# HGRN heads: six groups of small-block products issued as one run behind the last decayed tile

## The chip, the cores and the metric

The kernel runs on one NeuronCore of a Trainium2 chip. The metric is the device time of one execution in microseconds; before the change it is the median of three runs, 1376.57 us (1376.02 to 1377.64).

## What is computed

A two-layer streaming encoder over 512 tokens of width 1024. Layer 0 mixes tokens with a gated DeltaNet, layer 1 with an HGRN2 gated linear recurrence, each followed by a squared-ReLU MLP of width 4096 and all of it in float32. The change is in the token mixer of layer 1:

```python
def _hgrn2_chunked(q, k, v, g):
    """S_t = diag(f_t) S_{t-1} + k_t v_t^T (k_t = 1 - f_t), o_t = S_t^T q_t.
    q,k,g (B,T,H,DK) with g = log f_t <= 0; v (B,T,H,DV). float32."""
...
    def step(S, xs):
...
        a_off = jnp.einsum('bhsik,bhsjk->bhsij', q_off, k_off)
        dec = jnp.exp(jnp.where(diag_mask[:, :, None],
                                gs[..., :, None, :] - gs[..., None, :, :], -jnp.inf))
        a_diag = jnp.einsum('bhsik,bhsjk,bhsijk->bhsij', qs, ks, dec)
```

There are 8 heads of 128 features. For each head a matrix `a` is wanted, which holds for every pair of tokens s <= t inside a chunk the product of q at t with k at s, each feature decayed by the forget gates between s and t. `o` is then `a` times v plus what the carried state S gives.

## The kernel before

Activations lie transposed, 128 features on the partitions and the 512 tokens along the free axis, and a head's 512 tokens are 4 chunks of 128 (`NC`).

**Projections.** All big products are "three-term" ones: weights and activations are split into a rounded high part and a low rest, and TensorE does hi*hi, hi*lo and lo*hi (lines 122 to 124, one output block of 128 x 512; lines 674 to 676 for v, with tokens on the partitions and 256 columns). The weights arrive by DMA (`weights`, L105), ScalarE casts the high part (L111) and VectorE subtracts the low one (L112).

**The HGRN stage** (`hgrn`, L595) goes through the heads in four pairs. While a pair's heads are worked (`hgrn_head`), the projections of the next pair (`hgrn_in`) and the output gates of an earlier one (`hgrn_gates`) are there to fill TensorE. Heads are written inside `high_priority(offset=3000)`. The order in which each engine gets its instructions is made when the kernel is built: a scheduler plays the program through with its own costs and gives each engine the ready instruction of highest priority. On the chip each engine runs its list in that order and waits at an instruction until its inputs are there.

**One head** (`hgrn_head`, L696). `g` holds the log gates. Two tiles `dk`, `dq` (four VectorE multiplies, L719) give products inside pairs of tokens. After a running sum over 64 tokens (L740), five levels (`HLEVELS`, block lengths 2, 4, 8, 16, 32) each make one decayed tile `e`: two VectorE subtracts (L747, L748), one exp on ScalarE (L749, recorded at L85), two VectorE multiplies (L750, L751). Left halves of the blocks carry k, right halves q, so that `e` against itself gives the cross products of one level.

For `dk`, `dq` and for the levels 2 to 16, `gram32` (L726) issues one group: 16 products of 128 x 32 by 128 x 32, one for each 32-token block of each chunk, which use a 32-column strip of the array (`tile_position`); float32 products show as two records each, so a group is 32 records. Each group is followed on VectorE by the masking multiply (L735) or a predicated copy into `ad` (L754). Level 32 issues a sixth group of 8 products (L760, 16 records) that ScalarE copies into `a` (L763). GpSimd copies `ad` into the diagonal blocks of `a` (L765). Each group takes a PSUM tile of its own from the ring `mb`, which has three.

Then `qf` and `kg`, the tiles decayed over whole 64-token blocks, are made (L769 to L779). L783 multiplies them for the cross of the two 64-token blocks of each chunk: four products with 64 columns of `kg` as the stationary side and 64 of `qf` as the moving one. ScalarE copies the result into `a` (L784). Scalings (L788), transposes (L791), the state updates (L796 to L803) and the outputs (L808, L810) follow. `ol`, the ring of work tiles from which `half`, `dk`, `dq`, the five `e`, `qf`, `kg` and `kt` come, has eight buffers.

**After the last pair** come a normalisation (`rstd_rows`, L183) and the output projection (`out_proj`, L821). Its first two weight tiles make four output blocks at once, three in the ring `pj` and the fourth in `mb`, and it takes the heads in order, so that only its last part needs head 7.

Of the kernel before, what the change touches and what calls it, by code (L numbers as in the profile page):

```python
# [15 lines left out]
ALU = mybir.AluOpType  # L16
PSUM = bass.MemoryType.PSUM

T, D, HID, NH, P = 512, 1024, 4096, 8, 128
NB = D // P  # L20
B = 32
MIX = {"ma": 2, "mb": 3}
NC = T // P
# [5 lines left out]
HLEVELS = (2, 4, 8, 16, 32)  # L29
# [3 lines left out]
class Net:  # L33
# [40 lines left out]
    def acc(self, shape=None):  # L74
        return self.pj.tile(shape or [P, T], F32, tag="pj", name=self.name("pj"))

    def after(self, i, prev):
        self.tc.add_manual_dep(
            i.ins, prev.ins.name,
            mybir.DependencyInfo(mybir.DependencyClass.NoSync, mybir.DependencyReason.DATA),  # L80
            reason="table order")

    def act(self, out, in_, func, **kw):

# [611 lines left out]
    def hgrn_head(self, h, kq, g, vt):  # L696
        nc, mm, ident = self.nc, self.nc.tensor.matmul, self.ident
        k, q = kq[:, 0], kq[:, 1]
        ck = lambda t, c: t[:, c * P:(c + 1) * P]
        hs = slice(h, h + 1)  # L700

        nc.gpsimd.tensor_scalar(out=g, in0=g, scalar1=1e-37, scalar2=self.oml[:, hs], op0=ALU.max, op1=ALU.mult)
        self.act(g, g, AF.Ln, bias=self.lb[:, hs])
        nc.scalar.activation(out=q, in_=q, func=AF.Copy, scale=self.oml[:, hs])
        tmp = lambda: self.work("ol", bufs=NH)
        gram = lambda: self.mix("gr", tag="mb")


        half = tmp()
        hv = half.rearrange("p (a n) -> p a n", a=2)  # L710
        gp = g.rearrange("p (n b) -> p n b", b=2)
        self.act(hv[:, 0], gp[:, :, 1], AF.Exp, scale=0.5)
        self.act(hv[:, 1], gp[:, :, 1], AF.Exp, scale=-0.5)
        dk, dq = tmp(), tmp()
        for dst, src, sg in ((dk, k, 0), (dq, q, 1)):
            d2, s2 = (t.rearrange("p (n b) -> p n b", b=2) for t in (dst, src))
            for b in (0, 1):
                e = nc.vector
                e.tensor_tensor(out=d2[:, :, b], in0=s2[:, :, b], in1=hv[:, (b + sg) % 2], op=ALU.mult)  # L719
        a = self.work("x" if h % 2 else "e")  # L720
        c4 = lambda t: t.rearrange("p (c t) -> p c t", c=NC)
        nc.gpsimd.memset(a, 0.0)
        blk = [slice(b, b + B) for b in range(0, P, B)]
        ad = self.work("wd" if h % 2 else "ud", [P, NC, B])

        def gram32(x, y):  # L726
            pa = self.mix("gr", [P, NC, B], tag="mb")
            for c in range(NC):
                for b in blk:
                    mm(pa[b, c], lhsT=ck(x, c)[:, b], rhs=ck(y, c)[:, b], start=True, stop=True,  # L730
                       tile_position=(0, b.start))
            return pa

        pa = gram32(dk, dq)
        nc.vector.tensor_tensor(out=ad, in0=pa, in1=self.dmask.unsqueeze(1).to_broadcast([P, NC, B]), op=ALU.mult)  # L735


        gc = g
        b64 = lambda t: t.rearrange("p (n s) -> p n s", s=64)
        nc.vector.tensor_tensor_scan(out=gc, data0=self.fresh, data1=g, initial=0.0, op0=ALU.mult, op1=ALU.add)  # L740

        for i, s in enumerate(HLEVELS):
            nb = T // (2 * s)
            v4 = lambda t: t.rearrange("p (n a s) -> p n a s", a=2, s=s)
            e = tmp()
            ref = v4(gc)[:, :, 0, s - 1:s].to_broadcast([P, nb, s])
            nc.vector.tensor_tensor(out=v4(e)[:, :, 0], in0=ref, in1=v4(gc)[:, :, 0], op=ALU.subtract)  # L747
            nc.vector.tensor_tensor(out=v4(e)[:, :, 1], in0=v4(gc)[:, :, 1], in1=ref, op=ALU.subtract)  # L748
            self.act(e, e, AF.Exp)  # L749
            nc.vector.tensor_tensor(out=v4(e)[:, :, 0], in0=v4(e)[:, :, 0], in1=v4(k)[:, :, 0], op=ALU.mult)  # L750
            nc.vector.tensor_tensor(out=v4(e)[:, :, 1], in0=v4(e)[:, :, 1], in1=v4(q)[:, :, 1], op=ALU.mult)  # L751
            if s < B:
                pa = gram32(e, e)
                nc.vector.copy_predicated(out=ad, mask=self.lmask[:, i + 1].unsqueeze(1).to_broadcast([P, NC, B]),  # L754
                                          data=pa)
                continue
            pa = self.mix("gr", [P, NC, B], tag="mb")
            for c in range(NC):
                for l, r in (blk[0:2], blk[2:4]):
                    mm(pa[l, c], lhsT=ck(e, c)[:, l], rhs=ck(e, c)[:, r], start=True, stop=True,  # L760
                       tile_position=(0, l.start))
            for l, r in (blk[0:2], blk[2:4]):
                nc.scalar.copy(out=c4(a)[l, :, r], in_=pa[l])  # L763
        for b in blk:
            nc.gpsimd.tensor_copy(out=c4(a)[b, :, b], in_=ad[b])  # L765


        qf, kg = tmp(), tmp()
        self.act(qf, gc, AF.Exp)  # L769
        last = self.work("last", [P, 2 * NC], bufs=2)  # L770
        egl = self.work("egl", [P, NC], bufs=2)
        nc.vector.tensor_copy(out=last, in_=b64(qf)[:, :, 63])
        lv = last.rearrange("p (c b) -> p c b", b=2)
        nc.vector.tensor_tensor(out=egl, in0=lv[:, :, 0], in1=lv[:, :, 1], op=ALU.mult)
        nc.vector.tensor_tensor(out=qf, in0=qf, in1=q, op=ALU.mult)
        nc.vector.tensor_tensor(out=b64(kg), in0=b64(gc)[:, :, 63:64].to_broadcast([P, 2 * NC, 64]), in1=b64(gc),
                                op=ALU.subtract)
        self.act(kg, kg, AF.Exp)
        nc.vector.tensor_tensor(out=kg, in0=kg, in1=k, op=ALU.mult)  # L779
        pa = gram()  # L780
        for c in range(NC):
            t = c * P
            mm(pa[0:64, t + 64:t + P], lhsT=kg[:, t:t + 64], rhs=qf[:, t + 64:t + P], start=True, stop=True)  # L783
        nc.scalar.copy(out=c4(a)[0:64, :, 64:P], in_=c4(pa)[0:64, :, 64:P])  # L784
        for t, half, n in ((kg, slice(0, 64), NC - 1), (qf, slice(64, P), NC)):
            v = c4(t)[:, 0:n, half]
            f = lv[:, 0:n, half.start // 64 ^ 1:(half.start // 64 ^ 1) + 1]
            nc.vector.tensor_tensor(out=v, in0=v, in1=f.to_broadcast([P, n, 64]), op=ALU.mult)  # L788
        pt = self.mix("pt", [P, NC - 1, P])
        for c in range(NC - 1):  # L790
            nc.tensor.transpose(pt[:, c], ck(kg, c), ident)  # L791
        kt = tmp()
        nc.scalar.copy(out=c4(kt)[:, 0:NC - 1], in_=pt)
        ps = self.mix("ps", [P, NC - 1, P])
        for c in range(NC - 1):
            mm(ps[:, c], lhsT=ck(kt, c), rhs=vt[:, c], start=True, stop=True)  # L796
        st = [None]
        for c in range(NC - 1):
            sn = self.work("s", [P, P], bufs=3)
            if c == 0:  # L800
                nc.vector.tensor_copy(out=sn, in_=ps[:, 0])
            else:
                nc.vector.scalar_tensor_tensor(out=sn, in0=st[c], scalar=egl[:, c:c + 1], in1=ps[:, c],  # L803
                                               op0=ALU.mult, op1=ALU.add)
            st.append(sn)
        po = self.mix("po")
        for c in range(NC):
            mm(ck(po, c), lhsT=vt[:, c], rhs=ck(a, c), start=True, stop=(c == 0))  # L808
            if c:
                mm(ck(po, c), lhsT=st[c], rhs=ck(qf, c), start=False, stop=True)  # L810
        on = self.on[h] = self.work("oh", bufs=NH)
        nc.scalar.copy(out=on, in_=po)
        self.square_into(h == 0, on, "v" if h >= NH - 1 else "g")
# [194 lines left out]
```

## Time and profile before

| what | value |
|---|---|
| median of three runs | 1376.57 us (1376.02 to 1377.64) |
| the profiled execution's own time | 1375.37 us |
| its span in the trace | 1373.3 us |
| mean granted TensorE clock | 0.996 |
| HGRN heads, start of the first group (L730) and of the last (L760) | 758.4 and 964.1 us |
| records of L730, L760, L783 | 1280, 128, 64 |

Times inside the trace are microseconds from the span's start, durations of single instructions in nanoseconds where it says so. PE is TensorE's matmul row, PEld its weight loads, DVE VectorE, ACT ScalarE, POOL GpSimd. In a timeline row the first number is the start, the second the length from the first start to the last end of the merged instructions, then engine, line, operation, output and inputs, shapes and the count; brackets hold the idle time of the engine before it and what ended it. Matmuls are pipelined: one of 512 columns shows about 400 ns, while the next starts some 230 ns after it. So what a thing costs TensorE is read from starts, not from lengths. In a row of a group of instructions, the numbers behind the bar are the busy time, the mean of one in ns, the idle time before them and what ended it.

### The profile page before, as it was taken

How to read it: one execution, taken by the hardware profiler on the slowest of the kernel's cores; microseconds unless marked ns; L12 is line 12 of the kernel's file. 1: busy time of each engine (PE TensorE's matmuls, PEld its weight loads, DVE VectorE, ACT ScalarE, POOL GpSimd, SP SyncE). 2: the span in 40 equal slices, each digit the busy share in tenths (PEclk: the TensorE clock that was granted, in tenths of full speed). 3: DMA queues.
4: the chain of work that ended last, by engine and by line, in shares of the span. 5: the costliest groups of instructions: out<-in, count | busy, mean ns of one | idle time of the engine just before them, and what ended most of it. 6: DMA issues, size and time to landing. Idle time of an engine off the chain costs nothing.

```text
span 1373.3 us, 24089 instructions
## 1 busy us (share of the span) xinstructions
PE 1354.3 (99%) x10092; PEld 1102.5 (80%) x10092; DVE 830.1 (60%) x1525; ACT 583.4 (42%) x1090; POOL 209.0 (15%) x231
## 2 busy tenths in 40 slices
PE   8999999999999999999999999999999999999997
PEld 6777777777888888888888788787788888888897
DVE  6987777764844444444473985769784444445453
ACT  5755455544434313233124666466533422313242
POOL 4011101110200120211221033031110021120232
PEclk9999999999999999999999999999999999999998
DMA  6121101023222232222221212121042222232232
GB/s 197 62 94 63 63 33 63 32 86 101 91 94 96 92 113 99 92 93 92 94 97 55 93 63 93 63 93 63 32 153 92 93 92 93 92 115 100 92 136 80
DMA packets 23500, 121.55 MB, mean 89 GB/s; under 512 B 3808, under 2 KB 7008, under 8 KB 9824
## 3 DMA queue, kind: packets, MB, share of 16 engines
q1 hardware_dynamic: 23392, 120.02, 25.3%
q8 instruction: 79, 1.29, 0.4%
q14 instruction: 29, 0.24, 0.0%
HBM read 117.91 MB, written 2.10 MB: 87 GB/s over the span
## 4 chain that ended last, share of the span: by engine, by line
PE 90%; DVE 4%; ACT 3%; issue 1%; DMA 1%; SPq 0%; POOL 0%; POOLq 0%; ACTq 0%; DVEq 0%
PE pj L122 25%; PE pj L123 25%; PE pj L124 25%; PE px L495 1%; PE pu L502 1%; PE pga L460 1%; PE gr L730 1%; DMA raw<-gdn_in 1%; ACT L91 1%; PE pw L560 1%; PE pj L676 1%; PE pj L675 1%; PE pj L674 1%; PE po L572 1%; DVE ol L719 1%
## 5 line engine op out<-in xcount | busy, mean ns | idle before, releaser
L112 DVE TENSOR_TENSOR wlo<-raw,whi 128x1024 fp32r<-128x1024 f32 (+2 forms) x217 | 290.9, 1355 | 167.2 <-ACT whi L111 164.9
L111 ACT CAST whi<-raw 128x1024 fp32r<-128x1024 f32 (+2 forms) x222 | 222.1, 1023 | 389.6 <-PE pj L123 381.9
L123 PE MATMUL pj<-yl,whi 128*128 128x512 f32 x960 | 384.8, 401 | 0.0
L122 PE MATMUL pj<-yh,whi 128*128 128x512 f32 x960 | 383.1, 399 | 0.8 <-ACT whi L111 0.8
L124 PE MATMUL pj<-yh,wlo 128*128 128x512 f32 x960 | 382.6, 399 | 0.0
L122 PEld LDWEIGHTS pj<-yh,whi 128*128 128x128 f32 x960 | 181.3, 189 | 37.4 <-ACT whi L111 2.0
L123 PEld LDWEIGHTS pj<-yl,whi 128*128 128x128 f32 x960 | 181.6, 189 | 35.8 <-issue 0.4
L124 PEld LDWEIGHTS pj<-yh,wlo 128*128 128x128 f32 x960 | 181.3, 189 | 36.1 <-issue 0.7
L123 PE MATMUL pj<-ol,whi 128*128 128x512 f32 x336 | 131.2, 391 | 0.0
L868 DVE TENSOR_TENSOR gate<-pj,rB 128x512 f32<-128x512 f32 x56 | 38.6, 691 | 148.2 <-PE pj L124 148.2
L122 PE MATMUL pj<-oh,whi 128*128 128x512 f32 x320 | 125.1, 391 | 0.0
L124 PE MATMUL pj<-oh,wlo 128*128 128x512 f32 x320 | 125.0, 391 | 0.0
L870 POOL TENSOR_TENSOR kd<-kd,gate 128x512 f32<-128x512 f32 x18 | 23.3, 1292 | 462.5 <-DVE gate L868 462.5
L854 ACT ACTIVATE z<-pj 128x512 f32<-128x512 f32 x64 | 38.0, 594 | 113.7 <-PE pj L124 109.6
L123 PEld LDWEIGHTS pj<-ol,whi 128*128 128x128 f32 x336 | 63.1, 188 | 12.9
L124 PEld LDWEIGHTS pj<-oh,wlo 128*128 128x128 f32 x320 | 60.2, 188 | 12.2
L122 PEld LDWEIGHTS pj<-oh,whi 128*128 128x128 f32 x320 | 60.1, 188 | 12.2
L124 PE MATMUL pj<-kq,wlo 128*128 128x512 f32 (+1 forms) x192 | 68.3, 356 | 0.5 <-DVE wlo L112 0.5
L123 PE MATMUL pj<-kq,whi 128*128 128x512 f32 (+1 forms) x192 | 68.3, 356 | 0.0
L122 PE MATMUL pj<-kq,whi 128*128 128x512 f32 (+1 forms) x192 | 68.0, 356 | 0.0
L162 POOL TENSOR_TENSOR sqacc<-sqacc,z 128x512 f32<-128x512 f32 x25 | 37.3, 1492 | 119.4 <-ACT z L160 115.2
L91 ACT ACT_TABLE_LOAD x37 | 47.5, 1283 | 1.4 <-PEq L1000 0.7
(342 smaller groups left out, 2056.1 us busy)
## 6 DMA issues: line engine op xcount, KB each, us to landing
raw<-down SPq DMA_DIRECT2D x36, 1024.0 KB, 4.8
raw<-up SPq DMA_DIRECT2D x32, 1024.0 KB, 4.8
raw<-gdn_in SPq DMA_DIRECT2D x14, 1024.0 KB, 4.9
raw<-hgrn_fq SPq DMA_DIRECT2D x8, 1024.0 KB, 4.7
raw<-gdn_out SPq DMA_DIRECT2D x4, 1024.0 KB, 5.0
raw<-hgrn_i SPq DMA_DIRECT2D x4, 1024.0 KB, 4.7
raw<-hgrn_gate SPq DMA_DIRECT2D x4, 1024.0 KB, 4.8
raw<-hgrn_out SPq DMA_DIRECT2D x4, 1024.0 KB, 4.7
```

The costliest lines, as they stand in the source:

```text
L91: i = self.nc.scalar.preload_act_table_set(name)
L111: self.nc.scalar.copy(out=hi[:, k], in_=raw[:, k])
L112: eng.tensor_tensor(out=lo[:, k], in0=raw[:, k], in1=hi[:, k].bitcast(F32), op=ALU.subtract)
L122: mm(o, lhsT=hi[:, k, c], rhs=yh, start=(k == 0), stop=False)
L123: mm(o, lhsT=hi[:, k, c], rhs=yl, start=False, stop=False)
L124: mm(o, lhsT=lo[:, k, c], rhs=yh, start=False, stop=(k == NB - 1))
L162: e.tensor_tensor(out=self.sq, in0=self.sq, in1=t, op=ALU.add)
L460: mm(pga[:, c - c2], lhsT=ck(k, c), rhs=kq[:, :, c * P:(c + 1) * P], start=True, stop=True)
L495: mm(px[b, c], lhsT=n[b, c, b], rhs=wd[b, c], start=True, stop=True, tile_position=(b.start, b.start))
L854: nc.scalar.activation(out=z, in_=out, func=AF.Relu)
L868: nc.vector.tensor_tensor(out=t, in0=out, in1=self.r2b, op=ALU.mult)
L870: e.tensor_tensor(out=self.h[c], in0=self.h[c], in1=t, op=ALU.add)
```

## The change

The products of `dk`, `dq` and those of the five `e` are no longer issued as each tile is ready. All decayed tiles are made first; then the six groups are issued in one run. The first product of the run (`lead`) waits for the last multiply of the last level (`last`, a true dependency); all others are ordered behind `lead` (an order without a semaphore). The results go to two PSUM tiles of the ring `mb`, the first four groups to one and the last two to the other, instead of six tiles. The masking multiply, the four predicated copies and the two ScalarE copies follow behind all of this in the program. The number of products is the same.

Apart from this, L783 takes all 128 columns of `kg` as stationary side instead of 64 and writes 128 rows; the 64 rows more are not read.

```diff
-    def after(self, i, prev):
+    def after(self, i, prev, kind=mybir.DependencyClass.NoSync):
...
-        pa = gram32(dk, dq)
-        nc.vector.tensor_tensor(out=ad, in0=pa, in1=self.dmask.unsqueeze(1).to_broadcast([P, NC, B]), op=ALU.mult)
...
-        for i, s in enumerate(HLEVELS):
+        pairs = [(dk, dq)]
+        for s in HLEVELS:
...
-            nc.vector.tensor_tensor(out=v4(e)[:, :, 1], in0=v4(e)[:, :, 1], in1=v4(q)[:, :, 1], op=ALU.mult)
-            if s < B:
-                pa = gram32(e, e)
-                nc.vector.copy_predicated(out=ad, mask=self.lmask[:, i + 1].unsqueeze(1).to_broadcast([P, NC, B]),
-                                          data=pa)
-                continue
...
+            last = nc.vector.tensor_tensor(out=v4(e)[:, :, 1], in0=v4(e)[:, :, 1], in1=v4(q)[:, :, 1], op=ALU.mult)
+            pairs.append((e, e))
+
+
+        pa = [self.mix("gr", [P, n, NC, B], tag="mb") for n in (4, 2)]
+        lead = None
+        for i, (x, y) in enumerate(pairs):
+            o = pa[i // 4][:, i % 4]
+            wide = i == len(pairs) - 1
             for c in range(NC):
...
+                for l, r in ((blk[0:2], blk[2:4]) if wide else zip(blk, blk)):
+                    m = mm(o[l, c], lhsT=ck(x, c)[:, l], rhs=ck(y, c)[:, r], start=True, stop=True,
+                           tile_position=(0, l.start))
+                    if lead is None:
+                        lead = m
+                        self.after(m, last, mybir.DependencyClass.Sync)
+                    else:
+                        self.after(m, lead)
+        nc.vector.tensor_tensor(out=ad, in0=pa[0][:, 0], in1=self.dmask.unsqueeze(1).to_broadcast([P, NC, B]),
+                                op=ALU.mult)
+        for i in range(1, len(HLEVELS)):
+            nc.vector.copy_predicated(out=ad, mask=self.lmask[:, i].unsqueeze(1).to_broadcast([P, NC, B]),
+                                      data=pa[i // 4][:, i % 4])
+        for l, r in (blk[0:2], blk[2:4]):
+            nc.scalar.copy(out=c4(a)[l, :, r], in_=pa[1][l, 1])
...
-            mm(pa[0:64, t + 64:t + P], lhsT=kg[:, t:t + 64], rhs=qf[:, t + 64:t + P], start=True, stop=True)
+            mm(pa[:, t + 64:t + P], lhsT=kg[:, t:t + P], rhs=qf[:, t + 64:t + P], start=True, stop=True)
```

More of the change, by code (lines that the diff above doesn't have):

```diff
@@ L75, in acc @@
         return self.pj.tile(shape or [P, T], F32, tag="pj", name=self.name("pj"))
-    def after(self, i, prev):
+    def after(self, i, prev, kind=mybir.DependencyClass.NoSync):
         self.tc.add_manual_dep(
-            i.ins, prev.ins.name,
-            mybir.DependencyInfo(mybir.DependencyClass.NoSync, mybir.DependencyReason.DATA),
-            reason="table order")
+            i.ins, prev.ins.name, mybir.DependencyInfo(kind, mybir.DependencyReason.DATA), reason="order")
     def act(self, out, in_, func, **kw):
@@ L724, in hgrn_head @@
         ad = self.work("wd" if h % 2 else "ud", [P, NC, B])
[L726 to L732, printed above, removed]
-        pa = gram32(dk, dq)
-        nc.vector.tensor_tensor(out=ad, in0=pa, in1=self.dmask.unsqueeze(1).to_broadcast([P, NC, B]), op=ALU.mult)
         gc = g
@@ L750, in hgrn_head @@
             nc.vector.tensor_tensor(out=v4(e)[:, :, 0], in0=v4(e)[:, :, 0], in1=v4(k)[:, :, 0], op=ALU.mult)
-            nc.vector.tensor_tensor(out=v4(e)[:, :, 1], in0=v4(e)[:, :, 1], in1=v4(q)[:, :, 1], op=ALU.mult)
-            if s < B:
-                pa = gram32(e, e)
-                nc.vector.copy_predicated(out=ad, mask=self.lmask[:, i + 1].unsqueeze(1).to_broadcast([P, NC, B]),
-                                          data=pa)
-                continue
-            pa = self.mix("gr", [P, NC, B], tag="mb")
-            for c in range(NC):
[L759 to L763, printed above, removed]
+            last = nc.vector.tensor_tensor(out=v4(e)[:, :, 1], in0=v4(e)[:, :, 1], in1=v4(q)[:, :, 1], op=ALU.mult)
[5 more added lines that the diff above has]
+            wide = i == len(pairs) - 1
+            for c in range(NC):
+                for l, r in ((blk[0:2], blk[2:4]) if wide else zip(blk, blk)):
[13 more added lines that the diff above has]
+            nc.scalar.copy(out=c4(a)[l, :, r], in_=pa[1][l, 1])
         for b in blk:
```

## The prediction

> **What bounds the kernel now.** I read the page first: the share of each engine, the granted clock, the chain that ended last.
>
> ```profile
> span 1373.3 us, 24089 instructions
> ...
> PE 1354.3 (99%) x10092; PEld 1102.5 (80%) x10092; DVE 830.1 (60%) x1525; ACT 583.4 (42%) x1090; POOL 209.0 (15%) x231
> ...
> PE 90%; DVE 4%; ACT 3%; issue 1%; DMA 1%; SPq 0%; POOL 0%; POOLq 0%; ACTq 0%; DVEq 0%
> ```
>
> TensorE has work from end to end, and the chain is 90% TensorE. So a piece taken off TensorE's list shows in the end time, unless TensorE then waits for somebody. Whether it will is read from the stage itself: the busy time while the first pair of heads is worked, between the second and the third, and while the last is worked (stretch, length, then PE, PEld, DVE, ACT, POOL, granted clock).
>
> ```profile
> 757.00:797.00 40.00, 39.42 (x538) 30.59 (x538) 38.54 (x91) 26.29 (x45) 8.62 (x11) 1.00 0.26 85
> 841.00:873.00 32.00, 32.00 (x189) 28.48 (x188) 10.82 (x12) 15.26 (x23) 4.10 (x4) 1.00 0.33 109
> 930.00:973.00 43.00, 41.65 (x534) 31.41 (x533) 40.62 (x96) 28.44 (x47) 8.20 (x9) 1.00 0.18 59
> ```
>
> The clock is full. TensorE has 39.42 of 40 us in the first pair, but VectorE nearly as much (38.54). The heads run at VectorE's pace, and projections fill TensorE around them. Between the second pair and the third it is otherwise: 32.00 of 32 us on TensorE, 10.82 on VectorE. There TensorE alone decides when the third pair's inputs are complete, so whatever it saves in the first two pairs brings that start forward. I take the same for the fourth pair's start at 930.
>
> Next, the groups themselves, over the whole HGRN stage.
>
> ```profile
> L730 PE MATMUL gr<-ol 128*32 128x32 f32 x1024 | 14.6, 198 | 1.8 <-DVE ol L751 1.8
> L730 PE MATMUL gr<-ol,ol 128*32 128x32 f32 x256 | 3.7, 199 | 0.3 <-DVE ol L719 0.2
> L760 PE MATMUL gr<-ol 128*32 128x32 f32 x128 | 3.6, 198 | 0.7 <-DVE ol L751 0.7
> ```
>
> Those are (1024 + 256) / 32 = 40 groups of L730 and 128 / 16 = 8 of L760, 48 in all. The waits in front of them are small: 1.8 + 0.2 + 0.7 = 2.7 us over 8 heads.
>
> **Part 1: six groups become one run.** What one group costs TensorE now, from starts in the timeline of PE:
>
> ```profile
> 765.50 0.40 PE L122 MATMUL pj<-yh,whi 128*128 128x512 f32 x1
> 765.73 0.40 PE L123 MATMUL pj<-yl,whi 128*128 128x512 f32 x1
> 766.06 0.46 PE L730 MATMUL gr<-ol 128*32 128x32 f32 x32
> 766.45 0.50 PE L124 MATMUL pj<-yh,wlo 128*128 128x512 f32 x1
> 766.78 0.40 PE L122 MATMUL pj<-yh,whi 128*128 128x512 f32 x1
> ```
>
> Undisturbed, projections start every 0.23 us (765.50 to 765.73). From 765.73 to 766.78 there are two projections and a group: 1.05 - 2 x 0.23 = 0.59 us for the group. Its 32 records start within 0.46 - 0.20 = 0.26 us (busy less the mean of one, 198 ns). So 0.33 us goes to entering and leaving: 0.10 late before the group, 0.13 behind its last start, 0.10 more in front of the second projection.
>
> One place of the trace has two groups back to back:
>
> ```profile
> 894.45 0.40 PE L122 MATMUL pj<-yh,whi 128*128 128x512 f32 x1
> 894.78 0.80 PE L730 MATMUL gr<-ol 128*32 128x32 f32 x64
> 895.51 0.50 PE L123 MATMUL pj<-yl,whi 128*128 128x512 f32 x1
> 895.85 0.40 PE L124 MATMUL pj<-yh,wlo 128*128 128x512 f32 x1
> ```
>
> 895.85 - 894.45 - 0.46 = 0.94 us for both, so the second added 0.35. That is the upper bound for a group inside a run, as the second there can still hold a wait for its own tile. The lower bound is the 0.26 us of its records. I take 0.27, near the lower end, because in the run only the first product waits. L760's group has half the records, but in two strips instead of four; I count it like the others.
>
> Now: 46 single places x 0.59 + 0.94 + 2.7 of waits = 30.8 us. Then: 8 x (0.59 + 5 x 0.27) = 15.5 us (15.1 at 0.26, 18.7 at 0.35). Saved: 15.3 us (12.1 to 15.7), before any new wait.
>
> The Trainium skill speaks against this: "TensorE: Matmul & The Clock Gate", section "Wait — 56ns, not 53.3ns?", says that starts of matmuls never come closer than about 25 ns, however few columns they have. By that, an estimate, a run of 5 x 32 + 16 = 176 records takes 4.4 us; with 0.33 for entering and leaving that is 0.85 more per head than the six groups and their waits now, and the change would lose about 7 us. The trace does not agree for these strips: 64 records take 0.73 us from first start to the next projection, 11.4 ns each.
>
> **Part 2: the new wait.** TensorE's list is fixed; all projections queued behind `lead` wait with it, and the projections' readers behind them. How far TensorE trails VectorE today, at the last level of the first head, how closely masking operations sit in VectorE's list, and when `a` is first read:
>
> ```profile
> 764.04 0.29 DVE L754 COPY_PREDICATED ud<-lmask,gr 128x128 f32<-128x128 uint8 x1
> 764.24 0.42 DVE L747 TENSOR_TENSOR ol<-v 128x256 f32<-128x256 f32 x1
> ...
> 768.95 0.42 DVE L751 TENSOR_TENSOR ol<-ol,kq 128x256 f32<-128x256 f32 x1
> ...
> 770.01 0.45 PE L760 MATMUL gr<-ol 128*32 128x32 f32 x16
> ...
> 776.55 0.61 PE L808 MATMUL po<-e,uw 128*128 128x128 f32 x4
> ```
>
> The last group starts 770.01 - 769.37 = 0.64 us behind its tile. The upper bound for the new wait: the list keeps the same projections ahead of the run as now ahead of L760. TensorE then gets there earlier by five groups (2.95 us) and the waits now in front (2.7 / 8 = 0.34). The tile is ready earlier only by the four VectorE operations that leave its way, 0.20 us each from start to start: 0.8. That leaves 2.95 + 0.34 - 0.64 - 0.8 = 1.85 us per head. The lower bound is zero: the list has put enough projections ahead.
>
> I take 0.4 us per head, 3.2 us in all. The order is planned with costs, and the trace shows how well they hold: 48 groups stand where their tile comes, with 0.06 us of wait in the mean. A planner that priced a group far under 0.59 us would have let TensorE fall behind by the difference at each of the later four levels; it fell behind from nothing at the first, where it waited, to 0.64 us at the last. So groups are planned at close to their cost, and without them the list will hold nearly as much work in projections. What remains is the wait that heads 0, 2, 4 and 6 have now at the first level, up to 0.5 us (1.8 us over five times), moved to `lead`, and the small lag that no longer covers it.
>
> **Part 3: what moves on the other engines.** The masking multiply and the four copies move behind the run on VectorE: the same five operations, 1.0 us by their pitch. Behind them are queued GpSimd's copies into `a`, and ScalarE's. The first readers of `a` (L808) come at 776.55 in the first head, 7.2 us behind the last tile and behind `kg`, the cross, the transposes and the states; that chain hides the move. If that cover went, L808 would wait by up to those 1.0 us a head. `kg` needs a buffer of `ol`: seven of eight now stay in use until the run has read them. It waits for the first group of the run, while VectorE has about as much less to do ahead of it. I cost this at nothing. No DMA moves.
>
> **Part 4: the cross over 128 columns.**
>
> ```profile
> 772.76 0.39 PE L122 MATMUL pj<-yh,whi 128*128 128x512 f32 x1
> 773.08 0.68 PE L783 MATMUL gr<-ol,ol 128*64 128x64 f32 x8
> 773.68 0.50 PE L123 MATMUL pj<-yl,whi 128*128 128x512 f32 x1
> 774.02 0.39 PE L124 MATMUL pj<-yh,wlo 128*128 128x512 f32 x1
> ...
> 840.72 0.39 PE L123 MATMUL pj<-yl,whi 128*128 128x512 f32 x1
> 840.95 0.38 PE L810 MATMUL po<-ol,s 128*128 128x128 f32 x2
> 841.09 0.48 PE L124 MATMUL pj<-yh,wlo 128*128 128x512 f32 x1
> 841.40 0.39 PE L122 MATMUL pj<-yh,whi 128*128 128x512 f32 x1
> ```
>
> Now: 774.02 - 772.76 - 0.46 = 0.80 us for 8 records. L810 uses the whole array: 841.40 - 840.72 - 0.46 = 0.22 us for 2 records, 0.11 each and no step for entering. Eight of these are 0.88 us: 0.08 more per head, 0.6 us lost in all. If half the moving columns took half the time, it would be 0.44 us, a gain of 2.9. I take the row as it is, since its weights have the 128 columns that the cross will have.
>
> **Part 5: the end of the stage.** Here TensorE's gain can run into VectorE's chain.
>
> ```profile
> 980.74 0.69 DVE L203 SCALAR_TENSOR_TENSOR rB<-z,z 128x512 f32<-128x512 f32 x1
> ...
> 985.14 0.69 DVE L826 TENSOR_TENSOR gate<-pj,rB 128x512 f32<-128x512 f32 x1 [3.71 <-PE pj L124]
> ```
>
> The factor that the output projection's results need is ready at 981.4; the first result comes at 985.1: 3.7 us of slack. Two heads' saving brings TensorE forward by 2 x (15.3 - 0.6 - 3.2) / 8 = 2.9 us. Head 7 itself gets later: the output projection's fourth block holds one of the three `mb` buffers, the run holds the other two, so the cross must wait until VectorE has emptied one, 0.5 to 2 us later than now by the 1.0 us of masking and its queue. 3.7 - 2.9 - (0.5 to 2) is +0.3 to -1.2; I take 0.8 us lost.
>
> **Sum.** 15.3 - 0.6 - 3.2 - 0.8 = 10.7 us off the profiled execution's 1375.4: 1364.7. The median of the runs shown, 1376.57, lies 1.2 above that execution, so 1365.9, rounded to 1366.0.
>
> **Rivals.**
> *The end eats the last pair's gain.* Head 7 is late by more than its slack, and all that the last two heads save (2.9) is lost with the 0.8: 10.7 - 2.9 = 7.8, or 1368.8. For it: VectorE has 40.62 of 43 us in that stretch. Against: TensorE has the output projection of seven heads as filler.
> *No change: the run is queued too early.* The list keeps the same projections ahead; every head waits 1.85 us: 15.3 - 0.6 - 14.8 - 0.8 = -0.9, or 1377.5. Against it stands how closely the groups follow their tiles today.
> *Slower: the same, and VectorE's freed time goes to weights.* VectorE is 96% busy in the first pair. If subtracts for the projections slide in between the levels, the last tile comes no earlier, and the 0.8 us are gone: 2.65 us per head, 21.2 in all, -7.3, or 1383.9. It becomes a loss once the wait at `lead` passes (15.3 - 0.6 - 0.8) / 8 = 1.74 us per head.
>
> **Chances.** Forecast 0.68, end 0.16, no change 0.09, slower 0.07. Of the last, 0.01 is for a run whose records keep a distance of 25 ns, the rule of the Trainium skill's page above, since the double group speaks against it. About 0.2% (2.8 us) is what a measurement of this kernel can tell from none, so faster 0.84, same 0.09, slower 0.07. Range: no wait at all gives 15.3 - 0.6 + 0.4 for the bound of 0.26 = 15.1, or 1361.5; a wait of 1.4 us per head gives 2.7, or 1373.9. So 1361 to 1374, with the gain of 2.9 on the cross left out below and no change and slower left out above.
>
> **What would show it.** In the profile of the changed kernel: one piece of 176 records per head, some 1.5 us from first to last start, and no small group between the levels; a wait of PE for L751 (or what is now called `last`) of 0.2 to 0.7 us per head in the waits; the cross about 0.9 us between projections; the heads starting earlier by 3 us at the second pair, 6 at the third, 8 at the fourth; L826 near 975 with less than 1.5 us of idle. The forecast is wrong if the run is split by projections, if the wait passes 1.7 us per head, or if TensorE shows new waits for weights (L112) or for L203.

## The result, and the profile after

The changed kernel takes 1382.87 us (median of five runs, 1381.87 to 1384.81); the kernel before took 1376.57 us in the runs beside it. The ratio is 1.005, with a 95% interval of 1.0039 to 1.0061. The change makes the kernel slower by 6.3 us; forecast were 10.7 us less. The profiled execution is one of 1382.87 us, with a span of 1380.9 us.

Line numbers of the changed kernel: the run is L750, the masking multiply L757, the four predicated copies L760. Up to L721 they are two lower than before (`dk` and `dq` at L717); the running sum is L727, the subtracts of a level are L735 and L736, and `e` is finished at L739; from L764 on they are the same.

The page of the kernel after: the same three lines, on the span, on the engines' busy time and on the shares of the chain.

```profile
span 1380.9 us, 24019 instructions
...
PE 1348.5 (98%) x10092; PEld 1106.8 (80%) x10092; DVE 830.9 (60%) x1525; ACT 583.8 (42%) x1090; POOL 203.0 (15%) x231
...
PE 84%; DVE 8%; ACT 5%; POOL 1%; issue 1%; DMA 1%; SPq 0%; POOLq 0%; ACTq 0%; DVEq 0%
```

TensorE is busy 5.8 us less (1354.3 before), so there is a saving. But the chain now goes through VectorE for 8% instead of 4%. The busy time by stretch, for the first pair, between the second and third, and for the last pair (which starts later now):

```profile
757.00:797.00 40.00, 37.54 (x540) 31.41 (x538) 38.71 (x90) 26.28 (x45) 6.66 (x9) 1.00 0.28 103
843.00:875.00 32.00, 31.77 (x193) 28.57 (x193) 13.14 (x18) 15.90 (x24) 4.44 (x4) 1.00 0.34 121
936.00:979.00 43.00, 39.12 (x525) 32.17 (x525) 40.65 (x96) 28.80 (x47) 6.65 (x9) 1.00 0.17 55
```

TensorE was nearly full in the pairs before (39.42 of 40, 41.65 of 43). Now it idles 2.5 and 3.9 us there, while VectorE is as busy as before. What it waits for, over the stage from 740 to 1020 us (engine, its instruction, what ended the wait; total, times, longest), after:

```profile
PE po L808 <- POOL x L765: 5.6, 4, 3.5
PE gr L783 <- DVE ol L779: 3.7, 5, 0.9
PE gr L750 <- issue: 3.6, 2, 1.8
PE gr L750 <- DVE ol L739: 2.2, 4, 0.6
```

and before:

```profile
PE gr L730 <- DVE ol L751: 1.8, 5, 0.5
PE gr L760 <- DVE ol L751: 0.7, 1, 0.7
```

Three new waits stand there: for GpSimd's copies into `a`, for `kg`, and one for "issue", for which no engine is named. All of TensorE's gaps over 0.12 us in this stage add up to 3.4 us before and 16.3 after.

The run itself does what was forecast where nothing disturbs it. First head, timeline of PE:

```profile
767.80 0.39 PE L122 MATMUL pj<-yh,wlo 128*128 128x512 f32 x1
768.79 0.46 PE L750 MATMUL gr<-ol,ol 128*32 128x32 f32 x32 [0.60 <-DVE ol L739]
769.06 1.56 PE L750 MATMUL gr<-ol 128*32 128x32 f32 x144
770.56 0.50 PE L120 MATMUL pj<-yh,whi 128*128 128x512 f32 x1
770.89 0.39 PE L121 MATMUL pj<-yl,whi 128*128 128x512 f32 x1
771.13 0.40 PE L122 MATMUL pj<-yh,wlo 128*128 128x512 f32 x1
771.36 0.39 PE L120 MATMUL pj<-yh,whi 128*128 128x512 f32 x1
772.60 0.66 PE L783 MATMUL gr<-ol,ol 128*128 128x64 f32 x4 [0.85 <-DVE ol L779]
```

From 767.80 to 770.89 there are two projections at 0.23 and the run: 2.63 us, of it 0.7 of waiting. Two heads have it without a wait, at 1.97 (2.19 less 0.22 for two output products beside it). The last row shows the next trouble: the cross comes 1.24 us behind a projection, because `kg` was late.

A ledger sums, between 745 and 1000 us, what stands between projections beyond their own pitch (0.23 us for 512 columns, 0.12 for 256), from starts in the timeline; outputs that stand beside a run or a cross are taken out of it at 0.11 us a record:

| | before | after |
|---|---|---|
| six groups, or the run, with their waits | 31.0 | 23.9 |
| the cross, with its waits | 6.6 | 12.2 |
| transposes, states, outputs, with their waits | 24.2 | 32.7 |
| sum | 61.8 | 68.8 |

The run gives 7.1 us, not 15.3; the cross takes 5.6 back and the rest 8.5. The 7.0 us of difference are nearly all of the 7.6 by which the span grew.

**Where the outputs' wait comes from.** Sixth head, GpSimd and then PE, after (L160 is an addition for a normalisation; L700, which was L702 before, scales the gates of the next pair):

```profile
907.69 2.10 POOL L160 TENSOR_TENSOR sqacc<-sqacc,z 128x512 f32<-128x512 f32 x1 [1.46 <-ACT z L158]
909.78 2.42 POOL L700 TENSOR_SCALAR v<-v,oml 128x512 f32<-128x512 f32 x1
912.16 1.27 POOL L765 COPY x<-wd 32x128 f32<-32x128 f32 x4
```

```profile
913.48 0.71 PE L808 MATMUL po<-x,uw 128*128 128x128 f32 x4 [3.48 <-POOL x L765]
```

Before, in the same head, the copies came first:

```profile
900.98 1.67 POOL L765 COPY x<-wd 32x128 f32<-32x128 f32 x4 [14.24 <-DVE wd L754]
...
904.35 6.08 POOL L702 TENSOR_SCALAR v<-v,oml 128x512 f32<-128x512 f32 x2
```

They come later for two reasons. What they copy was complete at 907.54 us instead of 900.92, and GpSimd's list then had L160 and one L700 in front of them, which took until 912.2. That the filling is complete later is so in every head. First head, VectorE, after; the last tile was ready at 768.74:

```profile
770.53 1.22 DVE L110 TENSOR_TENSOR wlo<-raw,whi 128x1024 fp32r<-128x1024 f32 x1
771.67 0.28 DVE L757 TENSOR_TENSOR ud<-gr,dmask 128x128 f32<-128x128 f32 x1
771.87 0.68 DVE L779 TENSOR_TENSOR ol<-ol,kq 128x512 f32<-128x512 f32 x1
772.47 0.29 DVE L760 COPY_PREDICATED ud<-lmask,gr 128x128 f32<-128x128 uint8 x1
772.66 1.22 DVE L110 TENSOR_TENSOR wlo<-raw,whi 128x1024 fp32r<-128x1024 f32 x1
773.80 0.29 DVE L760 COPY_PREDICATED ud<-lmask,gr 128x128 f32<-128x128 uint8 x1
...
774.80 0.29 DVE L760 COPY_PREDICATED ud<-lmask,gr 128x128 f32<-128x128 uint8 x1
```

Five operations with a pitch of 0.2 us are spread over 3.4, since weight subtracts (L110) and the next steps stand in between. The end of L765, counted from the last tile, was 1.6 to 5.8 us before and is 7.3 to 12.5 us after, over the eight heads. The last tile itself comes sooner behind a head's start, 11.6 us instead of 12.5 in the first; the first output comes later, at 777.65 instead of 776.55.

### The profile page after: what moved, and what is told of

Same layout as the page of the kernel before. It is cut to its first block, busy times and chain, and to the rows that moved or that the text cites. A ratio compares the mean times of both kernels' runs of the same rounds, so it can differ in the third digit from the quotient of the medians.

```text
span 1380.9 us, 24019 instructions
## 1 busy us (share of the span) xinstructions
PE 1348.5 (98%) x10092; PEld 1106.8 (80%) x10092; DVE 830.9 (60%) x1525; ACT 583.8 (42%) x1090; POOL 203.0 (15%) x231
## 4 chain that ended last, share of the span: by engine, by line
PE 84%; DVE 8%; ACT 5%; POOL 1%; issue 1%; DMA 1%; SPq 0%; POOLq 0%; ACTq 0%; DVEq 0%
PE pj L122 24%; PE pj L121 24%; PE pj L120 24%; ACT L89 1%; PE px L493 1%; PE pu L500 1%; DVE wlo L110 1%; PE pga L458 1%; ACT whi L109 1%; DVE ol L717 1%; PE pw L558 1%; DVE ol L736 1%; DVE ol L739 1%; DVE ol L738 1%; DVE ol L735 1%
## 5 line engine op out<-in xcount | busy, mean ns | idle before, releaser
L110 DVE TENSOR_TENSOR wlo<-raw,whi 128x1024 fp32r<-128x1024 f32 (+2 forms) x217 | 290.7, 1352 | 162.8 <-ACT whi L109 160.5
L160 POOL TENSOR_TENSOR sqacc<-sqacc,z 128x512 f32<-128x512 f32 x25 | 38.0, 1519 | 126.1 <-ACT z L158 121.9
```

Of the source, the lines that this page charges most:

```text
L110: eng.tensor_tensor(out=lo[:, k], in0=raw[:, k], in1=hi[:, k].bitcast(F32), op=ALU.subtract)
L160: e.tensor_tensor(out=self.sq, in0=self.sq, in1=t, op=ALU.add)
```

## Experiments

Theory A: the run saves what was forecast, but TensorE's order is fixed; freed of the groups it reaches its next dependent products earlier, while what these need (the filling of `a`'s diagonal blocks, and `kg`) became later, and it waits. Rivals: B, the cross over 128 columns is the loss; C, the heads' pace through VectorE is the bound, so that a wait that is removed comes back elsewhere; D, beside A, the run outruns the supply of TensorE's own instructions. All times are medians; "before" was run beside each and lay between 1375.7 and 1376.4 us. Added lines shift the line numbers of some variants by two or three.

**The two parts alone.** e1 is the kernel before with the new cross; e2 is the changed kernel with the old cross.

> The kernel before with only the cross over 128 rows. Theory A (the run itself saves what was forecast; the time was lost again to three waits of TensorE: for kg in front of the cross, for the filled diagonal blocks in front of the first output product, and for its own instructions): the cross costs 0.1 us more per head, so 0.8 us in all and 1377.4. Theory B (the wider cross is what made it slower, since it pushes everything behind it in the head): 6 us, 1382 or more.

> The changed kernel with the cross back at 64 rows, so the run alone. Theory A: 0.8 us below the changed kernel, 1382, with the same waits in the trace. Theory B: 1376 or less.

e1: 1377.25 us, ratio 1.0008 (0.9999 to 1.0017). e2: 1382.42 us, 1.0041 (1.0027 to 1.0055). e1 lies where A put it (1377.4; B 1382 or more), and so does e2 (1382; B 1376 or less). B has fallen: the loss is the run's.

**GpSimd's order (e3).** The changed kernel, with the next pair's L700 ordered behind the last L765 of the pair before:

```diff
+        i = nc.gpsimd.tensor_scalar(out=g, ...)
+        if h > 1:
+            self.after(i, self.filled)
```

> The changed kernel, and GpSimd's scaling of the next pair's gates is ordered behind the four copies into the diagonal blocks of the pair before. Theory A: the waits of the first output product of heads 1, 3 and 5 for GpSimd (0.9, 0.8 and 3.7 us of TensorE's time) go, the one of head 7 (1.3) stays: 5 us less, 1378. Theory C (TensorE was only early; a wait taken away there comes back at the next place, because the heads' chain through VectorE and ScalarE sets the pace): no change, 1383.

1380.04 us, 1.0028 (1.0017 to 1.0038): 4.0 us above the kernel before beside it, where the changed kernel was 6.3 above. The waits for L765 fell from 5.6 to 2.7 us. That is half of what A said: GpSimd's list is a part of the loss.

**A buffer of its own for `kg` (e4).**

```diff
-        qf, kg = tmp(), tmp()
+        qf, kg = tmp(), self.work("z", bufs=3)
```

> The changed kernel with kg in a buffer of another ring (three buffers, nearly unused in this stage), so that it need not wait until the run has read dk. Theory A: the waits in front of the cross (5.1 us of TensorE's time over five heads) shrink to under 1 us, 4 us less, 1379. Theory C: no change, 1383. A third outcome, the same wait in front of the cross, would say that kg was late for VectorE's list and not for the buffer.

1389.72 us, 1.01 (1.0086 to 1.0114), 7 us worse than the changed kernel. PE's waits:

```profile
PE gr L750 <- issue: 6.1, 3, 2.2
PE po L808 <- POOL e L765: 5.0, 3, 3.2
PE po L808 <- POOL x L765: 3.6, 1, 3.6
PE gr L750 <- DVE ol L739: 2.6, 4, 0.8
PE gr L783 <- DVE z L779: 1.8, 2, 1.1
```

The crosses' waits for `kg` fell from 3.7 us to 1.8, so the buffer was most of their cause; but what follows the cross came earlier with it, and the outputs then waited 5.0 + 3.6 = 8.6 us for the filling. In the first head the fourth predicated copy now stood behind the next head's first operations, at 778.39. A missed (1379), and so did C (1383, no change). That a removed wait comes back elsewhere speaks for C, as long as the filling is late.

**Where the instruction waits stand (e5, e6).** In the sixth head of the changed kernel:

```profile
901.02 0.46 PE L750 MATMUL gr<-ol,ol 128*32 128x32 f32 x32
901.30 1.55 PE L750 MATMUL gr<-ol 128*32 128x32 f32 x142
904.69 0.22 PE L750 MATMUL gr<-ol 128*32 128x32 f32 x2 [1.85 <-issue]
```

The run stops for 1.85 us before its last product, though all its inputs are there. Counted over TensorE's weight loads, matmuls and semaphore instructions from the program's start, the last one before the stop is number 58 x 256 + 193. In all kernels here, every stop of TensorE longer than 1 us for which no engine is named stands directly behind a number that is 193 modulo 256. In the changed kernel, e5 and e6 a packet on the queue for instructions ends 1.3 to 1.6 us before each of these stops does. A product is four instructions, so a run has 352, which can hold a whole block of 256. Small products at the start of the program (57 of them in e5, 32 in e6) shift the count by 228 or 128:

```diff
+        for _ in range(57):
+            nc.tensor.matmul(warm[0:32, 0:32], lhsT=zeros[:, 0:32], rhs=zeros[:, 0:32], start=True, stop=True)
```

> The changed kernel with 57 small products (228 instructions for TensorE) more at the very start, where TensorE waits for its first data. The two gaps of 2.0 us inside the runs of heads 5 and 6 stand, like those in the other variants, at instructions whose number is 193 modulo 256. Theory D (they are TensorE waiting for its own instructions, which come in blocks of 256; a run of 352 holds a whole block when it starts 98 to 193 instructions into the count): with 228 more no run does, both gaps go, 4 us less, 1379. Rival E (a wait for a buffer or another engine that the trace does not name): the gaps stay at heads 5 and 6, 1383.

> The same with 32 small products (128 instructions). Theory D: the runs of heads 2 and 3 now hold a whole block and get a gap of 2 us each, those of heads 0 and 1 stand on the edge (block limits at their 3rd and first instruction) and probably get one too; heads 5 and 6 have none. Two to four gaps in place of two: 1383 to 1387. Rival E: gaps at heads 5 and 6 and nowhere else, 1383.

e5: 1386.2 us, 1.0069 (1.0056 to 1.0083); e6: 1392.6 us, 1.0115 (1.0102 to 1.0129). Both times missed what D said (1379, and 1383 to 1387). The padding itself takes 3.8 us at the start of e5, and the first run starts 3.8 us later than in the changed kernel (3.9 in e6). In e5 the stops inside the runs of the sixth and seventh heads are gone; one remains behind a run, again at 193:

```profile
PE pj L122 <- issue: 1.3, 1, 1.3
```

In e6 they stand in the third and fourth heads, where the shifted count says; of the first two heads, which D had on the edge, only the second has one, of 0.35 us:

```profile
820.95 1.37 PE L752 MATMUL gr<-ol 128*32 128x32 f32 x132
824.18 0.38 PE L752 MATMUL gr<-ol 128*32 128x32 f32 x12 [1.86 <-issue]
...
840.21 1.51 PE L752 MATMUL gr<-ol 128*32 128x32 f32 x140
843.77 0.25 PE L752 MATMUL gr<-ol 128*32 128x32 f32 x3 [2.06 <-issue]
```

D holds for the place of the stops, which E had fixed to the sixth and seventh heads. For the time, take the stretch from the last round of additions behind the first layer's MLP (its first starts at 692.86 us in the changed kernel, at 696.62 in e5) to the start of the last addition behind the second layer's output projection: e5 takes 327.1 us and the changed kernel 328.2. Of the 3.6 - 1.3 = 2.3 us of stops that are gone, half came back as other waits. In e6 the moved stops cost more than their length: the third pair's first run starts 10.4 us later than in the changed kernel, and the outputs' waits for the copies grew from 5.6 to 7.3 us. Why it is so much more stays open.

**Two runs (e7, e8).** Four groups behind level 8's tile, two behind level 32's; e8 also has the old cross.

```diff
+            if i in (0, 4):
+                lead, last = None, ready[2 if i == 0 else 4]
```

> The changed kernel with two runs per head in place of one: the first four groups behind the third level's tile, the last two behind the fifth's. One entering and leaving more per head, 0.33 us, 2.6 in all. Theory A and D: no run holds 256 instructions, so no gaps for instructions (4 us less); the filling of the diagonal blocks starts two levels earlier on VectorE and GpSimd, and the buffers of dk, dq and three levels are free sooner, so most of the 6.7 us in front of the output products and the 5.1 us in front of the cross go: 1383 + 3 - 4 - 8 = 1374, 2 us better than the kernel before. Theory C (the heads' own chain sets the pace): 1380 or more.

> Two runs per head and the cross back at 64 rows. 0.8 us less than with 128 rows, as the cross alone showed: 1373. If the difference lies within a microsecond either way, the order that the scheduler makes matters more than the 0.1 us per head.

e7: 1386.45 us, 1.0075 (1.0062 to 1.0089); e8: 1384.88 us, 1.0057 (1.0045 to 1.007). A and D had put them at 1374 and 1373, and missed; C had put e7 at 1380 or more. In e7 eight of the leads wait (4.4 us in all), the outputs still wait 6.7 us for the filling, and three instruction stops of 0.5 to 1.2 us remain, in the second runs.

**The filling, shortened or moved (e9, e10, e17).** e9: L765's copies on ScalarE. e10: the filling in three VectorE operations. e17: both.

```diff
-            nc.gpsimd.tensor_copy(out=c4(a)[b, :, b], in_=ad[b])
+            nc.scalar.copy(out=c4(a)[b, :, b], in_=ad[b])
...
+        nc.vector.tensor_tensor(out=m4, in0=pa[0], in1=self.fmask..., op=ALU.mult)
+        nc.vector.tensor_reduce(out=ad, in_=m4.rearrange("p i c t -> p c t i"), axis=mybir.AxisListType.X, op=ALU.add)
+        nc.vector.copy_predicated(out=ad, mask=self.lmask[:, 4]..., data=pa[1][:, 0])
```

> Theory A (the filling of the diagonal blocks is late, so the first output product L808 waits): with the four copies into `a` (L765) on ScalarE instead of GpSimd, they no longer stand behind L160 and the next pair's L700, so the waits of L808 for L765 in the odd heads (3.5 us in head 5, 2.1 in all in heads 1 and 7) fall under 1 us in all; 1379.5 us (1377 to 1382), as with the GpSimd order of the earlier run. Theory C (the heads' chain through VectorE sets the pace, a wait removed comes back at the next dependent product): the waits of L808 fall, but those of the crosses (L783) grow by as much, 1383 us (1381.5 to 1385).

> The five dependent VectorE operations that fill the diagonal blocks (masking multiply, four predicated copies) become three: one multiply of the run's whole first PSUM tile by float masks, one sum over its four groups, one predicated copy. Work on VectorE about the same or 1 us per head more, but only three places where weight subtracts can slide in. Theory A: the filling is complete 2 to 3 us earlier behind the last tile, L808's waits fall from 5.6 to about 2 us; 1379.5 us (1376 to 1383). Theory C: 1383 us (1381.5 to 1386).

> e10 (filling in three operations) with L765's copies on ScalarE. If e10's loss came from GpSimd copies that were held up while VectorE ran without a pause, the 8.6 us wait of head 0 goes: 1381 us (1378 to 1384). If it came from the three operations themselves (their longer VectorE work), 1390 us (1387 to 1394).

e9: 1381.32 us, 1.0039 (1.0027 to 1.0051). L808's waits for the copies are gone, the instruction stops grew from 3.6 to 5.9 us. The time is within A's range, but only 0.8 us nearer to the kernel before than the changed kernel is, which the intervals do not tell from nothing. e10: 1393.85 us, 1.0128 (1.0115 to 1.0141), far off what either theory said. One row of GpSimd and one of PE tell why:

```profile
775.54 11.10 POOL L767 COPY e<-ud 32x128 f32<-32x128 f32 x4 [21.66 <-DVE ud L763]
```

```profile
786.70 1.01 PE L810 MATMUL po<-e,uw 128*128 128x128 f32 x3 [8.61 <-POOL e L767]
```

Two of the four copies took 3.8 and 6.2 us instead of 0.29, beside VectorE going through the next head's levels without a pause. e17 has the same filling without GpSimd: 1380.52 us, 1.003 (1.002 to 1.004), so the loss was these copies. The Trainium skill, "SBUF — State Buffer", section "Who interferes with whom", has a rule for it: a VectorE instruction with two inputs in SBUF and a GpSimd instruction that reads SBUF share a port, and the later one is held up entirely. The stretched copies agree with that; no run here tried VectorE with one input.

**The filling left out (e11, e12).** The four predicated copies are dropped; e12 has the rest of the filling on ScalarE.

```diff
-        for i in range(1, len(HLEVELS)):
-            nc.vector.copy_predicated(out=ad, mask=self.lmask[:, i]..., data=pa[i // 4][:, i % 4])
```

> Leaves out the four predicated copies (levels 2 to 16 are multiplied but not put into `a`): the filling is the masking multiply alone. Theory A: filling complete by 4 us or less behind the last tile in even heads, no L808 wait for it there; what remains are GpSimd's list in heads 5 and 7, waits at the leads 2.2, crosses about 4, instructions 4; 1378 us (1375 to 1380). Theory C: 6.5 us of VectorE's work gone, but the waits turn up at the crosses and leads, idle of TensorE between 740 and 1022 still over 13 us; 1382 us (1380 to 1384).

> Leaves out the same four predicated copies and has L765's copies on ScalarE: nothing of the filling is left to wait for. Theory A: no wait of L808 above 0.5 us in any head; what remains are leads 2.2, crosses 4 to 5, instructions 4, so TensorE's idle between 740 and 1022 is about 10 us; 1376 us (1373 to 1378.5). Theory C: idle still over 13 us, 1381 us (1379 to 1384).

e11: 1378.19 us, 1.0015 (1.0007 to 1.0024), as A said: 2.4 us above the kernel before beside it, where the changed kernel was 6.3 above, so 3.9 us less, and below C's range. The outputs' waits for the copies (L805 here) fell from 5.8 to 0.4 us, while those at the leads and the crosses grew a little; so the gain comes from the filling. It includes the time of the copies themselves on VectorE, four operations a head with a pitch of 0.2 us; the kernel before without them wasn't run. What is left in e11, whose lines are three lower (the cross is L780):

```profile
PE gr L750 <- issue: 4.1, 2, 2.2
PE gr L780 <- DVE ol L776: 3.9, 5, 0.9
PE gr L750 <- DVE ol L739: 2.9, 5, 0.6
...
PE po L805 <- POOL e L762: 0.4, 1, 0.4
```

e12: 1380.1 us, 1.0031 (1.0019 to 1.0043), a miss for A and within C's range, with gaps of 14.8 us as C said: a third run met an instruction stop (5.6 us in all), and a projection waited 1.3 us for VectorE.

**Both causes at once, and controls (e13 to e16, e18).** e13 is e11 with `kg` in the ring `z`; e14 the kernel before with only that; e15 is e9 with it; e16 has it with e3's order and the odd head's L717 ordered behind the even head's last L760; e18 is e17 with it.

> Leaves out the four predicated copies as e11 did, and takes `kg` from the ring `z` as e4 did. In e4 the earlier cross was paid back by a later filling; here nothing of the filling is left that could be late. Theory A (filling and kg's buffer are the two causes): e11's cross waits of 3.9 us go and do not come back, 1374.5 us (1372 to 1376.5), below the kernel before. Theory C (the heads' pace through VectorE is the bound, a wait removed comes back elsewhere): 1378 us (1376.5 to 1381), idle of TensorE between 740 and 1022 still 11 us or more.

> Control: the kernel before with `kg` from the ring `z` and nothing else. `kg` had its buffer in time there, so no theory expects a gain: 1376 us (1374.5 to 1377.5) by A and C. If it gains 2 us or more, a gain of e13 is the buffer's own and not the run's.

> Everything computed; L765's copies on ScalarE and `kg` from the ring `z`. Theory A: cross waits go as in e4, the fillings no longer stand in GpSimd's list, but VectorE's five operations may still be strung out behind the next head's first operations: 1381 us (1377 to 1387). Theory C: 1385 us (1382 to 1390).

> Everything computed; `kg` from the ring `z`, the next pair's L700 ordered behind the last L765 of the pair before (as e3), and the odd head's four L717 ordered behind the last L760 of the even head, so that the filling cannot fall behind the next head on VectorE as it did in e4. Theory A: the even heads' L808 waits of e4 (3.2 and 3.6 us) fall under 1 us, 1379 us (1375 to 1383). Theory C: the odd heads start later by what the even heads gain, 1386 us (1382 to 1392).

> The same and `kg` from the ring `z`: everything computed, filling shortened and off GpSimd, cross waits removed. Theory A: 1378 us (1375 to 1382), between e13 (1375.6, filling left out) and e15 (1380.2, filling in five). Theory C: no better than e15, 1381 us or more.

| | us | ratio to before |
|---|---|---|
| e13 | 1375.58 | 1.0001 (0.9992 to 1.001) |
| e14 | 1379.32 | 1.003 (1.0018 to 1.0042) |
| e15 | 1380.21 | 1.0039 (1.0024 to 1.0054) |
| e16 | 1380.39 | 1.0041 (1.0027 to 1.0054) |
| e18 | 1386.34 | 1.0075 (1.006 to 1.009) |

e13 is the changed kernel without its loss: from 6.3 us above before to 0.15 below, 3.9 of it by the filling (e11) and 2.6 by `kg` (the intervals of e11 and e13 overlap slightly, so the second is the less sure). From the kernel before it can't be told apart, although it leaves out work. The time is in A's range, but the gaps still add up to 11.4 us, where C put them. In its waits:

```profile
PE gr L750 <- issue: 3.4, 2, 1.9
PE gr L750 <- DVE ol L739: 2.6, 4, 0.7
PE pj L674 <- issue: 1.3, 1, 1.3
PE gr L780 <- DVE z L776: 1.3, 2, 0.7
```

e14 shows that the buffer alone gains nothing; before, it costs 3.6 us, as L808 then waits 2.9 us for GpSimd. So e13's gain needs the run. e15 and e16 compute everything and stay 4.5 and 4.7 us above before, within A's ranges and below C's, though their intervals overlap the changed kernel's, each with 5.9 to 7.0 us of instruction stops in three heads. e18 missed: the three-operation filling takes a buffer of `z` as well, `kg` waits again (in the first head it comes at 774.45 instead of 769.65 in e15), and there are four stops (8.5 us). No variant beats the kernel before.

## Why the prediction was wrong

- **Part 1 was right in mechanism and in the price of a clean run**: 1.97 us in two heads, against 0.59 + 5 x 0.27 = 1.94. The other six cost more: 2.2 us of waits at `lead`, 3.6 of instruction stops in two runs, which no step foresaw, and some 1.6 where the last head's run was broken by outputs. The groups, 31.0 us, were put at 30.8. The rule of 25 ns between starts (the Trainium skill, "TensorE: Matmul & The Clock Gate", "Wait — 56ns, not 53.3ns?") plays no part: 144 records start in 1.56 - 0.20 = 1.36 us, 9.5 ns each.
- **Part 2 was right**: 2.2 us of wait at `lead` over the stage, against 3.2.
- **Part 3 is the step that failed**: "I cost this at nothing", with a chain of 7.2 us as cover. First, the five operations were given their pitch, 1.0 us, as if they would stand together; they depend on the run, which comes late, and stand in VectorE's list among weight subtracts. Second, GpSimd's list was not looked at: behind a later `ad`, L160 and the next pair's L700 come first. The filling ended 7.3 to 12.5 us behind the last tile and passed the cover; leaving its copies out returns 3.9 us, the copies' own time on VectorE included. Third, `kg`: that VectorE has less to do ahead of it does not help, since a buffer of `ol` comes free only with the run's first group; with the filling out of the way, its own buffer returns 2.6 us.
- **Part 4 was right**: an unwaited cross took 0.89 to 0.90 us (0.88 forecast), and e1 shows no measurable difference from before (1377.25 us beside 1376.06).
- **Part 5 was not reached**: L826 started at 992.6, not near 975, with 2.5 us of idle; the last pair itself began at 938.14 instead of 931.39. The heads were to start 3, 6 and 8 us earlier at the second, third and fourth pair; they started 2.6, 1.0 and 6.8 us later.
- **Of the rivals**, the slower one came near the time (1383.9) by luck, through another mechanism: it put 2.65 us on each head at `lead`, where 0.3 were measured. That freed time on VectorE "goes to weights" did happen, but behind the run, where it spread the filling.
- **What would show it** asked for waits at L751, L112 and L203 alone; the waits came at L808 and L783, which the list did not name.

What stays open: e13, with the two late inputs gone, still gains nothing over before. Its gaps are 8.0 us more than before's 3.4, and the four rows shown for it (stops, leads, crosses) make up 8.6 of its 11.4, which is most of the missing gain; but as half of the stops removed in e5 came back elsewhere, and e7 and e12 came out where C put them, C may hold for what is left. Whether a kernel with neither late input nor stop would get below 1376 us wasn't tried, since the padding that moves the stops costs more than they do.

## What to carry to other kernels

Work that is bundled behind its last input saves the engine that does it, but everything behind the bundle gets later by the whole collection; so price the readers' chain from the bundle's end, through every queue with its other entries in between, and not by the pitch of the operations. If the freed engine runs a fixed order, its saving shows only as far as those readers are ready; remove one late input and look for the next before counting a gain. A long run of very short instructions has its own bound, the supply of instructions.

## What the runs showed of the hardware

- **Instruction blocks.** TensorE's instructions come in packets of 256, 16 KB each: in the sixth head, between 902.30 and 903.30 us, the instruction queue moved one packet of 0.02 MB, and the stop ended at 904.69. A run of 352 instructions takes 1.97 us. Where an unbroken run passed the place 193 modulo 256 twice, TensorE stopped there the second time for 1.7 to 2.6 us, in all kernels here but for one run of e6, which began at 191. When that place came soon behind a run, the stop was 0.4 to 1.3 us. The last head's run in the changed kernel, drawn out to 3.9 us by output products, passed it twice without such a stop. The Trainium skill, "Runtime: NRT & Kernel Launch", section "Instruction fetch mechanics", has the blocks of 256 and says that fetching them is hidden, as instructions issue more slowly than blocks arrive. The size agrees with the counts here; that it is hidden doesn't hold for these runs of products of 32 columns.
- **GpSimd beside VectorE.** A copy of 32x128 takes 0.29 us at its shortest and took up to 6.2 us beside a VectorE that never paused (e10); before the change, one took 3.6 us.
